# Low-part matmuls at the end of each block, 15 KB more of small tiles, and a ninth early expert chunk in a two-layer diffusion backbone

## The chip, the cores and the metric

The kernel runs on one core of a Trainium2 chip. The metric is the device time of one execution in microseconds. Matmuls run on TensorE (PE in the profile, its weight loads PEld), elementwise work on VectorE (DVE), ScalarE (ACT) and GpSimd (POOL); SyncE (SP) issues every transfer between device memory and the on-chip SBUF. Each engine works through its own queue in order and waits on semaphores for the others.

## The reference

Two layers over 256 latent tokens and 256 context tokens of width 1024. Cut to what matters here:

```python
def _layer(x, xc, sc, sc_ctx, p, lambda_init, ctx_out):
    mod = split(sc @ p['w_mod'] + p['b_mod'], 6)               # modc likewise for the context
    h  = modulate(rmsnorm(x,  p['norm1_g']), mod[0],  mod[1])
    hc = modulate(rmsnorm(xc, p['norm1_g']), modc[0], modc[1])
    y, yc = token_mixer(h, hc, p, lambda_init, ctx_out)
    x = x + mod[2] * y
    x = x + mod[5] * ec_moe(modulate(rmsnorm(x, p['norm2_g']), mod[3], mod[4]), p)
    ...                                                        # the context alike, in layer 0 only
def token_mixer(h, hc, p, lambda_init, ctx_out):
    dq, dk, dv, hy, sq, sk, sv, gt = split_in(h @ p['w_in'])   # w_in: 1024 x 10752
    ...          # differential attention, Hyena long convolution, windowed attention
    return merge([y_diff, y_hy, y_swa], gt, p)
def merge(ys, gate_pre, p):
    gs = split(sigmoid(gate_pre), 3)
    merged = sum(gs[b] * (ys[b] @ p['w_branch'][b]) for b in range(3))
    return merged @ p['w_out']
def ec_moe(h, p):                                              # 16 experts, each takes its 32 best tokens
    aff = softmax(h @ p['router_w'])
    g, idx = top_k(swapaxes(aff, 1, 2), 32)
    xg = h[idx]
    a, b = xg @ p['moe_w1'], xg @ p['moe_w3']
    return scatter_add(idx, (silu(a) * b) @ p['moe_w2'] * g)
```

All values are fp32. An expert has three matrices of 1024 x 1024, so a layer reads 16 x 3 x 4 MiB = 201 MB of expert weights.

## The kernel before

Each layer has a mixer stage and an expert stage.

**Mixer.** `run_blocks` (L998) works through 116 blocks a layer: 84 of w_in (128 output columns each), 24 of w_branch and 8 of w_out. A block's weights come as one raw tile of 512 KB (`load_block`, L971). `split_block` (L976) makes two tiles in TensorE's fast fp32 form out of it: `wh`, the rounded high part, by ScalarE, and `wl`, the remainder. GpSimd makes the second half of `wl` at once; VectorE's half (`rest`, L984) is held back in a list, `later`, and put into VectorE's queue towards the end of the block before. The activations are split likewise into `hi` and `lo` (`hhi`, `hlo` for w_in, `yb` for a branch, `mg` for w_out). The product of a block is the sum over eight k-tiles of three matmuls: `wh` with `hi`, `wh` with `lo`, `wl` with `hi` (`mm3`, L460). Every matmul loads its own stationary tile. 512 columns stand for latents and context, 256 for the latents alone, which most blocks of layer 1 need.

**Background.** The three token mixers, the modulation vectors and others are generators that a planner (`Background`, L287) puts between the matmuls of the blocks. When the program is built, a model keeps a clock for each engine; `pump` (L367) hands over the next background step when the model says that its operands are ready and a credit allows it, `until` (L383) does so while the model says that TensorE would wait for the tiles named, and `drain` forces a group to its end where a branch needs it. So the order of every engine's queue is fixed at build time. `LATER` (L39) says from which k-tile on a block releases the next block's `rest` and may request a further raw tile; a raw tile is requested ahead only while more than `SPARE` tiles of 4 KB are free (L1040).

**Experts.** The weights come in 96 chunks a layer of 2 MB (`fill`, L1664), in the order in which `prod` (L1829) consumes them, into seven tiles of 16 KB. Four of the first chunks are requested during the last mixer blocks of layer 0 (`PREF`, L46). Chunks named in `extra` (L1654) go into tiles of 4 KB and 2 KB that are free only at the start of the stage: chunk 4 into four of 4 KB (5 in layer 1), chunk 7 into three of 4 KB and two of 2 KB. The later ones wait until `prod` has used up a chunk.

**Memory.** `BUFS` (L58) holds the number of tiles of each size: a16 is 16 KB per partition, a4 4 KB, a2 2 KB, a1 1 KB. The program object reserves 16 KB per partition for descriptors of transfers that GpSimd issues.

Of the kernel before, what the change touches and what calls it, by code (L numbers as in the profile page):

```python
# [21 lines left out]
KT = 8  # L22
T = 256
L = 2
# [11 lines left out]
COST = {"setup": 500.0, "filter": 60000.0, "mod": 15000.0, "modA": 5000.0, "modN": 5000.0, "diff": 9000.0, "hy": 10000.0, "swa": 4000.0, "post": 1000.0}  # L36
CREDIT = (3000.0, 4000.0)
SLACK = 200.0
LATER = (6, 4)  # L39
SPARE = (1, 1)  # L40
EARLY = 1
FILTER_E = 4
# [12 lines left out]
ORDER = ("dddd" + "hhd" * 2 + "hhhh" + "dd", "dh" * 4 + "dddd")  # L55
PI_IN = 3.1415925
SWAP = list(range(16, 32)) + list(range(16))
BUFS = {"a16": 7, "a8": 3, "a4": 10, "a2": 8, "a1": 3, "t": 6, "s": 24, "t2": 1}  # L58


def constants():
# [347 lines left out]
class Kernel:  # L409
# [24 lines left out]
    def sb(self, tag, shape, dt=F32, name="w"):  # L434
        self.cnt += 1
        t = self.pool.tile(shape, dt, name=f"{name}_{self.cnt}", tag=tag, bufs=BUFS[tag])
        self.model.tile(t, tag, BUFS[tag])
        return t
# [559 lines left out]
    def run_blocks(self, bl, ahead=2, first=3):  # L998
        nl = ns = first
        later = []  # L1000
        for j, b in enumerate(bl):
            self.bg.due, end = [], self.bg.now
            for c in bl[j:]:
                if c.drains:
                    self.bg.due.append((c.drains, end))
                end += 24 * (4.0 + 0.41 * c.n)
            while ns < min(max(j + ahead, first + (j > 0)), len(bl)):
                self.split_block(bl[ns], later if j else None)
                ns += 1
            while nl < len(bl) and (nl <= ns or (nl - ns < 3 and self.model.dead("a4", BUFS["a4"]) > SPARE[self.bg.layer])):  # L1010
                self.load_block(bl[nl])
                nl += 1
            if self.bg.layer and len(bl) - 1 - j == MODR:
                self.bg.add("mod", lambda task: self.mod_vec([(1, v) for v in range(3, 6)]))
            if j < first:
                while later:
                    later.pop(0)()
                if j == 0:
                    for c in bl[:first]:
                        if c.pre:  # L1020
                            c.pre()
                    hi, lo = b.hl()
                    ps = [self.bank([128, c.n], "d" if i < 2 else "b") for i, c in enumerate(bl[:first])]
                    for k in range(KT):
                        self.bg.until([hi[:, k], lo[:, k]])
                        for c, p in zip(bl, ps):
                            self.mm3(p, (c.wh[:, k], c.wl[:, k]), (hi[:, k, 0:c.n], lo[:, k, 0:c.n]), k == 0, k == KT - 1)
                b.wh = b.wl = None
                b.evac(ps[j])
                continue  # L1030
            if b.pre:
                b.pre()
            hi, lo = b.hl()[:2]
            p = self.bank([128, b.n], "d")
            for k in range(KT):
                self.bg.until([b.wh[:, k], b.wl[:, k], hi[:, k], lo[:, k]])
                self.mm3(p, (b.wh[:, k], b.wl[:, k]), (hi[:, k, 0:b.n], lo[:, k, 0:b.n]), k == 0, k == KT - 1)
                if k >= LATER[self.bg.layer] and later:
                    later.pop(0)()
                if k > LATER[self.bg.layer] and nl < len(bl) and nl - ns < 3 and self.model.dead("a4", BUFS["a4"]) > SPARE[self.bg.layer]:  # L1040
                    self.load_block(bl[nl])
                    nl += 1
                if k < KT - 1:
                    self.bg.pump()
            b.wh = b.wl = None
            if len(bl) - 1 - j in PREF[self.bg.layer]:
                self.fill(PREF[self.bg.layer][len(bl) - 1 - j])
            b.evac(p)
            self.bg.pump()
# [21 lines left out]
    def clear(self, n):  # L1071
        while self.model.dead("a2", BUFS["a2"]) < n:
            self.bg.force()

    def room(self, **need):
        def gate():
            return all(self.model.dead(tag, BUFS[tag]) >= n for tag, n in need.items())
        return gate
# [547 lines left out]
    def moe(self, l):  # L1626
        nc, A = self.nc, self.A
        nq = 4 if l < L - 1 else 2
        ns = nq // 2
# [21 lines left out]
        self.mw = []  # L1651
        self.held, self.live = 0, deque()
        full = 6 if l < L - 1 else 7
        extra = {4: (4, 0, 1), 7: (3, 2, 2)} if l < L - 1 else {5: (4, 0, 1), 7: (3, 2, 2)}  # L1654

        def row(c, k):
            return c[:, k] if len(c.shape) == 3 else c[:, k // c.shape[2], k % c.shape[2]]
# [400 lines left out]
```

## Time and profile before

| | |
|---|---|
| median of 3 runs | 2607.61 us (2601.46 to 2608.32) |
| profiled execution | 2600.63 us, its span 2598.8 us |
| TensorE busy | 2244.1 us (86%), granted clock 0.943 on average |
| VectorE, ScalarE, GpSimd busy | 1338.3 (51%), 884.2 (34%), 793.6 us (31%) |
| transfers | 590.31 MB, 227 GB/s on average |

The page shows the whole execution; shares of busy time are averages over the stages, so the stages have to be read one by one. A row of the timeline gives an instruction's start and length and, in brackets, how long its engine was idle before it and who ended that. Matmuls are pipelined: the distance from one start to the next is their price, the length shown is more. The granted clock is the share of 2.4 GHz that TensorE was given; it has two levels, 2.4 and 1.2 GHz.

### The profile page before, as it was taken

The page shows a single profiled execution, that of the slowest core. Times are in us where ns is not written, and L with a number is a line of the kernel's source. Part 1 is how long each engine was busy: PE and PEld are TensorE (multiplying, and loading weights), DVE is VectorE, ACT ScalarE, POOL GpSimd, SP SyncE. Part 2 cuts the span into 40 slices and gives each one's busy share as a digit, 9 for nine tenths or more (in the row PEclk, how much of TensorE's full clock was granted, in tenths as well). Part 3 has the DMA queues.
Part 4 walks back from the last instruction along what each step waited for, and adds up shares of the span by engine and source line. Part 5 has one row for each costly group of instructions (what it writes and reads, how often), then busy time and mean ns, then how long its engine had stood idle before and what let it go on. Part 6 is the DMA issues. An engine that isn't in the chain of part 4 may idle for free.

```text
span 2598.8 us, 38727 instructions
## 1 busy us (share of the span) xinstructions
PE 2244.1 (86%) x14970; PEld 1539.4 (59%) x14970; DVE 1338.3 (51%) x2907; ACT 884.2 (34%) x1933; POOL 793.6 (31%) x775
## 2 busy tenths in 40 slices
PE   6999998999989998999998898988989887656565
PEld 4777776777768775333433377877877773223223
DVE  4777788788772324223333268778887541101011
ACT  4444444565552332101111154545544431000001
POOL 2644335642234540000111155664454430000000
PEclk8999999999999999999999999999999988788787
DMA  8443333221213367899999942322466689999997
GB/s 296 117 126 115 98 114 106 65 57 50 58 57 90 98 251 304 366 427 414 396 408 391 398 145 83 112 82 74 121 180 187 174 297 410 425 424 422 423 424 304
DMA packets 325983, 590.31 MB, mean 227 GB/s; under 512 B 45948, under 2 KB 278056, under 8 KB 297896
## 3 DMA queue, kind: packets, MB, share of 16 engines
q1 hardware_dynamic: 325800, 587.84, 61.8%
q8 instruction: 118, 1.93, 0.3%
q14 instruction: 65, 0.53, 0.1%
HBM read 584.66 MB, written 3.15 MB: 226 GB/s over the span
## 4 chain that ended last, share of the span: by engine, by line
PE 51%; DMA 22%; DVE 18%; ACT 3%; issue 3%; POOL 1%; SPq 1%; DVEq 0%; ACTq 0%; POOLq 0%
PE p L458 48%; DMA mw<-in_moe_w_dram 20%; DVE arena L261 6%; DVE t L261 4%; PE p L469 3%; DVE wl L261 2%; DMA wm<-in_w_mod_dram 2%; DVE qp L261 1%; SPq L261 1%; DVE yb L261 1%; ACT wh L261 1%; ACT arena L261 1%; DVE ma L261 1%; DVE yc L261 1%; ACT qp L261 1%
## 5 line engine op out<-in xcount | busy, mean ns | idle before, releaser
L458 PE MATMUL p<-mw,xg 128*32 128x256 f32 (+1 forms) x3072 | 412.4, 509 | 116.4 <-DMA mw<-in_moe_w_dram 114.0
L458 PE MATMUL p<-hhi,wl 128*128 128x512 f32 (+1 forms) x1344 | 480.4, 357 | 24.9 <-DVE wl L261 24.4
L458 PE MATMUL p<-hhi,wh 128*128 128x512 f32 (+1 forms) x1344 | 495.3, 369 | 7.2 <-ACT wh L261 4.1
L458 PE MATMUL p<-hlo,wh 128*128 128x512 f32 (+1 forms) x1344 | 476.4, 354 | 2.1 <-POOL hlo L261 1.3
L261 POOL TENSOR_TENSOR wl<-wraw,wh 128x512 fp32r<-128x512 f32 x232 | 343.0, 1479 | 392.2 <-ACT wh L261 320.7
L458 PEld LDWEIGHTS p<-mw,xg 128*32 128x32 f32 (+1 forms) x3072 | 133.1, 129 | 320.5 <-issue 201.8
L458 PEld LDWEIGHTS p<-hhi,wl 128*128 128x128 f32 x1344 | 258.6, 192 | 73.0 <-DVE wl L261 38.3
L458 PEld LDWEIGHTS p<-hhi,wh 128*128 128x128 f32 x1344 | 259.5, 193 | 43.9 <-issue 8.9
L458 PEld LDWEIGHTS p<-hlo,wh 128*128 128x128 f32 x1344 | 259.7, 193 | 30.0 <-POOL hlo L261 2.2
L261 ACT ACTIVATE wh<-wraw 128x1024 fp32r<-128x1024 f32 x232 | 242.4, 1053 | 50.8 <-DMA wraw<-in_w_in_dram 14.6
L458 PE MATMUL p<-mw,aT 128*32 128x256 f32 (+3 forms) x1760 | 197.1, 461 | 60.8 <-DMA mw<-in_moe_w_dram 57.9
L261 DVE TENSOR_TENSOR wl<-wraw,wh 128x512 fp32r<-128x512 f32 x231 | 198.6, 860 | 74.8 <-ACT wh L261 68.4
L261 ACT ACTIVATE arena<-p 128x512 f32<-128x512 f32 (+1 forms) x212 | 107.1, 509 | 374.2 <-PE p L458 290.3
L458 PE MATMUL p<-yb,wh 128*128 128x512 f32 (+1 forms) x768 | 196.7, 346 | 0.1
L458 PEld LDWEIGHTS p<-mw,aT 128*32 128x32 f32 (+1 forms) x1760 | 75.8, 128 | 171.3 <-issue 99.3
L261 DVE COPY yS<-p 32x512 f32<-32x512 f32 (+1 forms) x60 | 33.4, 556 | 268.9 <-ACT yS L261 268.9
L261 POOL TENSOR_TENSOR sq<-sq,sq 128x512 f32<-128x512 f32 (+1 forms) x6 | 6.3, 1055 | 506.4 <-ACT sq L261 502.9
L458 PE MATMUL p<-yb,wl 128*128 128x512 f32 (+1 forms) x384 | 133.0, 346 | 23.6 <-DVE wl L261 22.7
L458 PEld LDWEIGHTS p<-yb,wh 128*128 128x128 f32 x768 | 133.1, 194 | 15.7 <-issue 1.0
L261 ACT ACTIVATE arena<-p,t 128x512 f32<-128x512 f32 (+1 forms) x192 | 116.5, 613 | 66.4 <-DVE t L261 60.3
L261 ACT ACTIVATE s<-p 128x512 f32<-128x512 f32 (+1 forms) x32 | 15.7, 491 | 344.1 <-PE p L458 344.0
L261 ACT ACTIVATE yS<-p 32x256 f32<-32x256 f32 (+2 forms) x84 | 35.3, 420 | 261.5 <-PE p L458 233.9
(243 smaller groups left out, 3523.7 us busy)
## 6 DMA issues: line engine op xcount, KB each, us to landing
mw<-in_moe_w_dram SPq DMA_DIRECT2D x173, 2048.0 KB, 20.4
wraw<-in_w_in_dram SPq DMA_DIRECT2D x152, 512.0 KB, 3.9
wm<-in_w_mod_dram SPq DMA_DIRECT2D x72, 512.0 KB, 4.4
mw<-in_moe_w_dram SPq DMA_DIRECT2D x40, 512.0 KB, 22.5
mw<-in_moe_w_dram SPq DMA_DIRECT2D x17, 1024.0 KB, 29.2
wraw<-in_w_branch_dram SPq DMA_DIRECT2D x32, 512.0 KB, 3.7
wm<-in_w_mod_dram SPq DMA_DIRECT2D x5, 2048.0 KB, 7.9
wraw<-in_w_in_dram SPq DMA_DIRECT2D x32, 256.0 KB, 3.4
```

The costliest lines, as they stand in the source:

```text
L261: return f(*args, **kw)
L458: self.nc.tensor.matmul(out, lhsT=lhsT, rhs=rhs, start=start, stop=stop, skip_group_check=tiles > 1)
L469: self.nc.tensor.transpose(out, in_, self.ident[:n, :n])
```

## The change

Five places of the code change.

```diff
-LATER = (6, 4)
+LATER = (10, 6)
...
-BUFS = {"a16": 7, "a8": 3, "a4": 10, "a2": 8, "a1": 3, "t": 6, "s": 24, "t2": 1}
+BUFS = {"a16": 7, "a8": 3, "a4": 13, "a2": 9, "a1": 4, "t": 6, "s": 24, "t2": 1}
...
-            for k in range(KT):
-                self.bg.until([b.wh[:, k], b.wl[:, k], hi[:, k], lo[:, k]])
-                self.mm3(p, (b.wh[:, k], b.wl[:, k]), (hi[:, k, 0:b.n], lo[:, k, 0:b.n]), k == 0, k == KT - 1)
-                if k >= LATER[self.bg.layer] and later:
+            for i in range(2 * KT):
+                k = i % KT
+                if i < KT:
+                    self.bg.until([b.wh[:, k], hi[:, k], lo[:, k]])
+                    self.mm(p, b.wh[:, k], hi[:, k, 0:b.n], i == 0, False)
+                    self.mm(p, b.wh[:, k], lo[:, k, 0:b.n], False, False)
+                else:
+                    self.bg.until([b.wl[:, k]])
+                    self.mm(p, b.wl[:, k], hi[:, k, 0:b.n], False, k == KT - 1)
+                if i >= LATER[self.bg.layer] and later:
                     later.pop(0)()
-                if k > LATER[self.bg.layer] and nl < len(bl) and nl - ns < 3 and self.model.dead("a4", BUFS["a4"]) > SPARE[self.bg.layer]:
+                if i > LATER[self.bg.layer] and nl < len(bl) and nl - ns < 3 and self.model.dead("a4", BUFS["a4"]) > SPARE[self.bg.layer]:
                     self.load_block(bl[nl])
                     nl += 1
-                if k < KT - 1:
+                if i < KT or k % 2 and k < KT - 1:
                     self.bg.pump()
...
-        extra = {4: (4, 0, 1), 7: (3, 2, 2)} if l < L - 1 else {5: (4, 0, 1), 7: (3, 2, 2)}
+        extra = {4: (4, 0, 1), 7: (3, 2, 2), 8: (3, 2, 2)} if l < L - 1 else {5: (4, 0, 1), 7: (3, 2, 2), 8: (3, 2, 2)}
...
-    nc = bacc.Bacc("TRN2", target_bir_lowering=False, num_devices=1)
+    nc = bacc.Bacc("TRN2", target_bir_lowering=False, num_devices=1, dynamic_dma_scratch_size=1024)
```

A block now has 16 steps instead of 8: eight of two matmuls with `wh`, then eight of one with `wl`. The release of the next `rest` moves from step 6 of 8 (after 21 of 24 matmuls) to step 10 of 16 (after 19) in layer 0, and from after 15 to after 14 in layer 1. `pump` is called after the first eight steps and after three of the last eight. The first three blocks of a layer, which run together, keep the old order.

TensorE's queue at the first block of a branch product in layer 0 (`p_4815`, in the changed program `p_4881`), before:

```order
L458 MATMUL p_4815<-yb_4760,wh_4756 128x512
L458 MATMUL p_4815<-yb_4761,wh_4756 128x512
L458 MATMUL p_4815<-yb_4760,wl_4757 128x512
...
L458 MATMUL p_4827<-kp_4382,qp_4720 128x256
L458 MATMUL p_4827<-kl_4383,qp_4720 128x256
```

and now (`yb_4829` is the high part of the branch's activations, `yb_4830` the low part; the `arena` and `cst` rows are background; left out are repeats of the two `wh` rows):

```order
L458 MATMUL p_4881<-yb_4829,wh_4823 128x512
L458 MATMUL p_4881<-yb_4830,wh_4823 128x512
L469 MATMUL p_4884<-cst_68,arena_575 128x128 x2
...
L458 MATMUL p_4907<-arena_575,arena_573 128x128 x2
...
L458 MATMUL p_4917<-arena_575,arena_574 128x128 x4
...
L458 MATMUL p_4881<-yb_4829,wl_4824 128x512 x6
L469 MATMUL p_4936<-cst_68,arena_574 128x128 x4
L458 MATMUL p_4881<-yb_4829,wl_4824 128x512 x2
```

The third matmul used `wl`; now the eight with `wl` stand at the end, and the matmul that reads `arena_573` comes after five pairs of `wh` matmuls. VectorE's queue at the same place, before:

```order
L261 TENSOR_TENSOR yb_4761<-arena_575,yb_4760 128x512
L261 TENSOR_TENSOR yb_4761<-arena_576,yb_4760 128x512 x3
L261 TENSOR_TENSOR wl_4757<-wraw_4542,wh_4756 128x512
L261 TENSOR_TENSOR qp_4720<-arena_574,qp_4720 64x128 x2
L261 TENSOR_REDUCE t_4838<-p_4827 128x1
```

and now:

```order
L261 TENSOR_TENSOR yb_4830<-arena_573,yb_4829 128x512
L261 TENSOR_TENSOR yb_4830<-arena_574,yb_4829 128x512 x2
L261 TENSOR_TENSOR yb_4830<-arena_573,yb_4829 128x512
L261 TENSOR_TENSOR wl_4824<-wraw_4557,wh_4823 128x512
L261 COPY arena_573<-p_4884 128x256
L261 RECIPROCAL t_4793<-t_4793 128x2
```

`wl` stands behind the four `yb` instructions in both; what follows it is other background work. SyncE's queue at the start of layer 0's expert stage, where `mw` are tiles of expert weights, before:

```order
L261 DMA mw_8935<-in_moe_w_dram 128x1024
L261 DMA mw_8939<-in_moe_w_dram 128x512
L261 DMA mw_8940<-in_moe_w_dram 128x512
L261 DMA mw_9095<-in_moe_w_dram 128x4096
L261 DMA mw_9105<-in_moe_w_dram 128x4096
```

and now:

```order
L261 DMA mw_8939<-in_moe_w_dram 128x512
L261 DMA mw_8940<-in_moe_w_dram 128x512
L261 DMA mw_8943<-in_moe_w_dram 128x1024
L261 DMA mw_8944<-in_moe_w_dram 128x1024
L261 DMA mw_8945<-in_moe_w_dram 128x1024
L261 DMA mw_8949<-in_moe_w_dram 128x512
L261 DMA mw_8950<-in_moe_w_dram 128x512
L261 DMA mw_9105<-in_moe_w_dram 128x4096
```

Chunk 8, one transfer into a tile that a used-up chunk has to free (`mw_9095`), became five into small tiles (`mw_8943` to `mw_8950`); chunk 9 now takes the first freed tile.

## Rows read from the trace of the kernel before

**Rows 1.** Table of stretches: start and end, length, busy us of each engine, clock, DMA.

```profile
41.00:780.00 739.00, 693.82 (x3893) 534.51 (x3892) 565.73 (x1263) 368.01 (x843) 322.83 (x346) 0.98 0.32 92
...
1510.00:2030.00 520.00, 462.94 (x3176) 406.98 (x3175) 409.65 (x804) 273.04 (x547) 276.16 (x245) 0.96 0.39 114
2130.00:2600.00 470.00, 299.10 (x3619) 142.29 (x3619) 67.01 (x187) 41.30 (x114) 2.85 (x4) 0.82 0.96 399
```

**Rows 2.** Costly groups of the page: busy, mean ns, idle before and its releaser.

```profile
L458 PE MATMUL p<-hhi,wl 128*128 128x512 f32 (+1 forms) x1344 | 480.4, 357 | 24.9 <-DVE wl L261 24.4
L458 PE MATMUL p<-yb,wl 128*128 128x512 f32 (+1 forms) x384 | 133.0, 346 | 23.6 <-DVE wl L261 22.7
```

**Rows 3.** Waits of TensorE, 41 to 985 us: total us, times, longest us.

```profile
PE p L458 <- DVE wl L261: 25.7, 23, 4.2
PE p L469 <- DVE arena L261: 3.5, 7, 1.2
```

**Rows 4.** Waits of TensorE, 1500 to 2130 us.

```profile
PE p L458 <- DVE wl L261: 21.4, 14, 3.9
PE p L469 <- DVE arena L261: 16.0, 16, 2.5
PE p L469 <- DVE yd L261: 13.7, 5, 4.2
PE p L458 <- ACT wh L261: 4.1, 2, 3.3
```

**Rows 5.** Timeline of TensorE, 748 to 756 us: start, length, instruction, idle before.

```profile
748.30 0.39 PE L458 MATMUL p<-hlo,wh 128*128 128x512 f32 x1
748.53 0.39 PE L458 MATMUL p<-hhi,wl 128*128 128x512 f32 x1
...
753.54 0.80 PE L458 MATMUL p<-yb,wl 128*128 128x512 f32 x1 [4.16 <-DVE wl L261]
754.13 1.05 PE L458 MATMUL p<-yb,wh 128*128 128x512 f32 x2
754.99 0.63 PE L458 MATMUL p<-yb,wl 128*128 128x512 f32 x1
```

**Rows 6.** Timeline of TensorE in layer 1, 2039 us.

```profile
2039.21 0.28 PE L458 MATMUL p<-hlo,wh 128*128 128x256 f32 x1
2039.33 0.28 PE L458 MATMUL p<-hhi,wl 128*128 128x256 f32 x1
```

**Rows 7.** Timeline of VectorE, then of TensorE, 519 to 526 us.

```profile
519.02 5.21 DVE L261 TENSOR_TENSOR yb<-arena,yb 128x512 fp32r<-128x512 f32 x4
524.15 1.75 DVE L261 TENSOR_TENSOR wl<-wraw,wh 128x512 fp32r<-128x512 f32 x1
...
525.96 0.54 PE L458 MATMUL p<-yb,wl 128*128 128x512 f32 x1 [3.44 <-DVE wl L261]
```

**Rows 8.** Table of stretches behind waits for wl, first and last.

```profile
274.00:277.00 3.00, 3.00 (x14) 1.24 (x13) 3.00 (x4) 1.45 (x4) 2.92 (x4) 0.50 0.57 176
...
2079.00:2082.00 3.00, 3.00 (x15) 3.00 (x16) 1.78 (x2) 0.00 (x0) 1.96 (x2) 0.56 0.99 243
```

**Rows 9.** DMA queues of the page: packets, MB, share of 16 engines' span.

```profile
q1 hardware_dynamic: 325800, 587.84, 61.8%
```

**Rows 10.** Table of stretches in the expert stages; last three numbers clock, DMA, GB/s.

```profile
1005.00:1010.00 5.00, 4.54 (x31) 4.00 (x31) 2.39 (x11) 0.00 (x0) 0.00 (x0) 0.50 0.97 404
1015.00:1020.00 5.00, 5.00 (x42) 2.40 (x40) 2.81 (x12) 2.56 (x8) 0.00 (x0) 1.00 0.01 3
2140.00:2145.00 5.00, 5.00 (x77) 2.98 (x78) 2.64 (x11) 2.77 (x8) 0.00 (x0) 0.92 0.02 5
2160.00:2165.00 5.00, 5.00 (x80) 3.20 (x73) 1.87 (x7) 1.39 (x4) 0.00 (x0) 1.00 1.00 424
```

**Rows 11.** Waits of TensorE for expert weights, 985 to 1500, then 2130 to 2600 us.

```profile
PE p L458 <- DMA mw<-in_moe_w_dram: 20.6, 21, 2.0
...
PE p L458 <- DMA mw<-in_moe_w_dram: 151.4, 80, 5.7
```

## Prediction

> **What bounds the kernel now.** I read the table of stretches first, with stretches cut where the program changes its work [rows 1]. The reader is to see two kinds. In the two mixer stretches (41 to 780 and 1510 to 2030 us) TensorE is busy 94% and 89% of the time, VectorE 77% and 79%, and the DMA engines a third: a mixer ends when TensorE's stream of matmuls ends, and VectorE is near enough behind it to hold it up. In an expert stretch (the second, 2130 to 2600 us) the DMA share is 0.96 while TensorE falls to 64%: there the weights' arrival sets the end.
>
> Then the page's list of costly groups, for what ended TensorE's idle time [rows 2]. The groups that read `wl`, the low part of a weight block, were preceded by 24.9 us of idle time in the w_in blocks and 23.6 us in the branch blocks, nearly all of it ended by VectorE writing `wl`. The lists of waits say where: 25.7 us in 23 waits before 985 us [rows 3], 21.4 us in 14 waits from 1500 to 2130 us [rows 4]; together 47.1 us, the longest 4.2 us. Last the timelines of single waits and the stretches behind them, for the clock and for what VectorE was doing.
>
> The sum below is made against the profiled execution's own 2600.63 us (a span of 2598.8 us and 1.83 us around it). That execution is 7.0 us under the median of the three runs, 2607.61 us, so I add 7 at the end.
>
> **The change part by part.**
>
> *Low-part matmuls last.* Counts stay: 24 matmuls a block, each with its own weight load, before and after. What moves is when `wl` is first needed. Before, it was the third matmul of a block; now it is the seventeenth, so 14 matmuls stand between. With 512 columns one starts every 0.23 us (748.30 and 748.53 us in [rows 5]), with 256 every 0.12 us [rows 6]: 3.2 us or 1.7 us of grace. The waits average 25.7/23 = 1.1 us and 21.4/14 = 1.5 us, so nearly every one is shorter than the grace it gets. VectorE's instruction for `wl` keeps its place behind the background work in its queue, so its end does not move.
>
> That bounds the gain at 47 us. The other bound is that VectorE is simply late: TensorE works in order, and once past `wl` it meets a background matmul that needs VectorE too. The branch block shown in the order listing tells how much. VectorE finished four `yb` instructions at 524.2 us and `wl` at 525.9 us; TensorE stood 3.44 us before the block's third matmul, until 525.96 us [rows 7]. In the new order the sixth pair is preceded by a matmul on `arena_573`, which VectorE copies right behind `wl`: TensorE gets 10 matmuls (2.3 us) into the block instead of 2, and about half of the wait is left there. So I take half of the branch blocks' 22.7 us, 11 us, and 70% of the w_in blocks' 24.4 us, 17 us, since those waits are shorter and a block of w_in has no `yb` instructions in front of its `wl`. Together **28 us**; bounds 12 (a quarter) and 47.
>
> *The clock behind those waits.* After seven of the waits the granted clock was at 1.2 GHz, half, for some microseconds; first and last of the seven are [rows 8], and the row at 753.54 us in [rows 5] shows it: after 4.16 us of waiting, two matmuls take 0.86 us, not 0.46. Seven stretches of 3 us (one of 6) with a mean clock near 0.52 lose about 24 x 0.48 = 11.5 us. Where the wait halves, the fall may still come: I take 60%, **7 us**; bounds 2 and 11.5. Where the clock falls elsewhere, I leave it.
>
> *More pump points and thresholds.* A block now hands over to the background tasks after 11 of its steps, before after 7, so the same background matmuls come in smaller portions and partly earlier. No instruction is added; I count zero here and put the risk into the rivals.
>
> *Small tiles.* 13, 9 and 4 tiles in place of 10, 8 and 3 of the sizes 4, 2 and 1 KB: 15 KB per partition, paid for by the scratch. Raw weight blocks can be requested earlier. TensorE waited 4.1 us for `wh` in two places in the second layer [rows 4], one of them 3.27 us with the clock halved behind it; an earlier request removes most: **3 us**; bounds 0 and 6.
>
> *Scratch of 1 KB.* All of the program's own transfers stand on one hardware queue [rows 9] and are issued by SyncE; GpSimd issues none. Nothing uses what is taken away: 0 us.
>
> *Ninth early chunk.* A chunk is 128 x 4096 fp32 = 2.10 MB; at the 424 GB/s that the queue reaches [rows 10] that is 4.95 us. Both expert stretches have a hole to put it in: the queue moved 3 GB/s from 1015 to 1020 us and 5 GB/s from 2140 to 2145 us, because every buffer was full [rows 10]. Filling it moves all later chunks forward by up to 4.95 us. In the second layer TensorE waits 151.4 us for these weights [rows 11], so the end follows in full. In the first it waits only 20.6 us, so a little is lost: 4 us. Together **9 us**; bounds 4.9 and 9.9. The chunk comes in five transfers (three of 512 KB, two of 256 KB) where the later ones are one of 2 MB. From 1005 to 1010 us, while two whole and two split chunks were being worked off, the queue still ran at 404 GB/s [rows 10], so I charge nothing for the splitting. The Trainium skill (SBUF — State Buffer, "The DMA setup-cost knee") speaks against the piece: a transfer pays about 2 us whatever its size, so the largest single transfer is to be preferred. By that rule four more transfers would cost an estimated 8 us each time if nothing hid them, 16 us in all, and the sum would come out at 2576 us; the 404 GB/s disagrees as long as transfers are queued behind each other.
>
> **Sum.** 28 + 7 + 3 + 9 = 47 us; 2600.6 - 47 = 2553.6, plus 7: **2560 us**. With all lower bounds, 12 + 2 + 0 + 5 = 19, it is 2589; with all upper ones, 47 + 11.5 + 6 + 10 = 74.5, it is 2533.
>
> **The rivals.**
>
> *The wait only moves.* If VectorE sets the pace of the mixers, all of the 47 us and the clock loss come back in front of background matmuls. For it: VectorE is 79% busy in the second mixer, and TensorE's other long waits there, 16.0 us for `arena` and 13.7 us for `yd` [rows 4], are already VectorE being late. Against it: in the first layer the waits for `arena` are 3.5 us [rows 3], so VectorE mostly catches up. Only the chunk and the raw loads stay: 2607.6 - 12 = 2596 us.
>
> *Slower.* The place is the mixers' background matmuls: with more pump points they may be put into TensorE's stream before their operand is ready, and everything behind stands. Its price is read from what they cost now: 3.5 us [rows 3] and 16.0 + 13.7 us [rows 4], 33.2 us. It decides from the point where the growth of these exceeds what `wl`, clock, raw loads and chunk give. If they grow by three quarters, 25 us, while the `wl` waits come back as well: 2596 + 25 = 2621 us. Against it speaks that the same number of matmuls is spread over more places, not bunched.
>
> *The ninth chunk buys nothing*, because the thirteen 4 KB tiles it needs are still held by the last w_out blocks, or TensorE's gather stands in the way. Then 47 - 9 = 38 us remain: 2569 us.
>
> *More than the sum.* The extra small tiles also let background tasks start earlier, and half of those 33.2 us go too, and some 8 us of half clock behind them: 2560 - 25 = 2535 us.
>
> **How the numbers follow.** Forecast 0.56, the wait only moves 0.16, slower 0.06, chunk without effect 0.14, more than the sum 0.08. The forecast's own range is 2533 to 2589 us. The range of 8 in 10 has to take in most of the first rival (2596) and leaves out the far ends: 2530 to 2602 us. A measurement of this kernel can tell about 0.3% from no change, here 7.8 us, so faster means under 2599.8 us. Faster is the forecast, the idle chunk, the larger gain and 0.09 of the moved wait: 0.87. Same is 0.07 of the moved wait and 0.01 of the slower case: 0.08. Slower is the remaining 0.05.
>
> **What would show it.** Right: TensorE's waits for `wl` fall from 47 us to under 15 us; its waits for `arena` and `yd` grow by less than 20 us; the stretches of half clock behind branch blocks' third matmul are gone; the first expert weight is needed some 30 to 40 us earlier in each profile's own time; in the few microseconds after each router the queue stays above 300 GB/s. The forecast is wrong in its main step if the `wl` waits vanish and the mixers are as long as before: then VectorE paced them. It is wrong in the chunk if the two expert stretches, measured from the first expert matmul to the end, are not shorter by 4 to 5 us each.

## The result and the profile after

The changed kernel takes 2577.82 us (median of 4 runs, 2572.00 to 2579.04) against 2605.77 us for the kernel before in the same comparison: a ratio of 0.9893, 95% interval 0.9878 to 0.9908. That is 28 us faster; forecast were 47 from the profiled time. The pair of profiles shows less, 2600.63 - 2579.04 = 21.6 us, because the profiled run of before was faster than all its timed runs and that of after was the slowest of its four.

First the stretches: before, then after, cut at the same points of the program (first block, first branch product, first w_out block of layer 0; the same for layer 1, there up to the last branch block). These four rows of before are finer than [rows 1].

```profile
41.00:522.00 481.00, 453.87 (x2471) 351.40 (x2471) 370.59 (x751) 226.14 (x483) 244.11 (x255) 0.97 0.37 111
522.00:940.00 418.00, 397.68 (x2128) 312.69 (x2127) 239.08 (x575) 186.45 (x422) 150.64 (x139) 0.99 0.26 75
1514.00:1814.00 300.00, 269.55 (x1681) 238.09 (x1682) 227.52 (x464) 164.34 (x319) 174.97 (x151) 0.98 0.32 90
1814.00:2093.00 279.00, 243.84 (x1898) 219.88 (x1898) 212.94 (x384) 130.95 (x263) 134.33 (x121) 0.94 0.58 165
```

```profile
42.00:526.00 484.00, 453.34 (x2488) 352.12 (x2488) 377.82 (x768) 233.27 (x502) 240.73 (x257) 0.98 0.37 111
526.00:933.00 407.00, 392.05 (x2111) 308.63 (x2110) 231.55 (x558) 179.50 (x403) 151.71 (x136) 1.00 0.28 81
1508.00:1787.00 279.00, 260.25 (x1643) 229.55 (x1642) 232.38 (x438) 157.76 (x302) 167.89 (x147) 0.99 0.33 95
1787.00:2071.00 284.00, 253.10 (x1937) 229.86 (x1936) 217.36 (x409) 135.09 (x280) 144.91 (x125) 0.92 0.57 163
```

Layer 0 gained 8 us (899 to 891), layer 1 16 us (579 to 563). Layer 1's w_in part gained 21 and its branch part lost 5. The counts of matmuls (x, first column) move between the parts: background work is shifted, so only a whole mixer can be compared.

The groups of after that answer to [rows 2], and two that grew (columns: busy, mean ns, idle before and its releaser):

```profile
L458 PE MATMUL p<-hhi,wl 128*128 128x512 f32 (+1 forms) x1344 | 312.9, 361 | 4.5 <-DVE wl L261 4.4
L458 PE MATMUL p<-yb,wl 128*128 128x512 f32 (+1 forms) x384 | 79.1, 343 | 0.1
L469 PE MATMUL p<-cst,arena 128*128 128x128 f32 x608 | 101.0, 290 | 28.8 <-DVE arena L261 27.8
L458 PE MATMUL p<-kp,qp 128*128 128x512 f32 (+1 forms) x192 | 75.3, 399 | 12.2 <-DVE qp L261 11.3 <-ACT arena L261 0.4
```

The waits for `wl` are gone: 4.4 us are left of 47.1. Where TensorE waits now, layer 0 (42 to 979 us) and then layer 1 (1494 to 2109 us), against [rows 3] and [rows 4]:

```profile
PE p L469 <- DVE arena L261: 10.2, 12, 3.0
PE p L458 <- DVE qp L261: 6.6, 9, 2.0
PE p L458 <- DVE arena L261: 6.4, 4, 3.0
PE p L458 <- POOL yb L261: 5.9, 9, 1.6
PE p L469 <- DVE yd L261: 3.2, 4, 1.7
...
PE p L469 <- DVE arena L261: 17.6, 16, 2.8
PE p L458 <- DVE arena L261: 8.2, 5, 3.3
PE p L469 <- DVE yd L261: 4.9, 2, 4.0
PE p L458 <- DVE qp L261: 4.7, 6, 2.3
PE p L458 <- DVE wl L261: 4.4, 4, 2.9
```

In layer 0 much of the 25.7 us came back before `arena`, `qp` and `yb`: TensorE's gaps over 0.3 us add up to 47 us before and 46 after. In layer 1 they fell from 64 to 47 us, `yd` alone from 13.7 to 4.9. At the block of [rows 7] two operands are late now: first `yb` itself, which I had not counted, and then, five pairs of matmuls into the block, the `arena` tile that I had argued with (timeline of TensorE, then VectorE's `wl`, after):

```profile
525.74 0.62 PE L458 MATMUL p<-yb,wh 128*128 128x512 f32 x2
...
526.34 0.48 PE L458 MATMUL p<-yb,wh 128*128 128x512 f32 x1
528.40 1.18 PE L458 MATMUL p<-yb,wh 128*128 128x512 f32 x4 [1.58 <-POOL yb L261]
530.10 0.97 PE L458 MATMUL p<-yb,wh 128*128 128x512 f32 x3 [0.52 <-POOL yb L261]
532.66 0.71 PE L458 MATMUL p<-arena,arena 128*128 128x128 f32 x4 [1.60 <-DVE arena L261]
...
530.52 1.76 DVE L261 TENSOR_TENSOR wl<-wraw,wh 128x512 fp32r<-128x512 f32 x1
```

The waits inside this block are 1.58 + 0.52 + 1.60 = 3.7 us, against 3.44 us before: here nothing of the wait is gained. The queue in the expert stages, answering to [rows 10] (last number GB/s): the hole behind each router is still there, and layer 0 has a second one.

```profile
1009.00:1014.00 5.00, 5.00 (x41) 2.40 (x42) 2.75 (x11) 2.52 (x8) 0.00 (x0) 1.00 0.02 5
1046.00:1051.00 5.00, 5.00 (x54) 3.50 (x52) 1.55 (x5) 1.28 (x4) 0.00 (x0) 0.97 0.00 0
1051.00:1056.00 5.00, 5.00 (x46) 2.45 (x43) 2.46 (x9) 2.23 (x8) 0.00 (x0) 1.00 0.00 0
2109.00:2114.00 5.00, 0.69 (x4) 0.23 (x4) 4.03 (x14) 0.42 (x1) 0.67 (x1) 0.50 1.07 425
2119.00:2124.00 5.00, 5.00 (x63) 2.91 (x64) 1.76 (x7) 1.86 (x7) 0.00 (x0) 0.75 0.03 7
```

At the second hole the kernel before still moved 59 and then 360 GB/s:

```profile
1052.00:1057.00 5.00, 5.00 (x57) 3.50 (x55) 1.55 (x5) 1.28 (x4) 0.00 (x0) 1.00 0.25 59
1057.00:1062.00 5.00, 5.00 (x46) 2.46 (x43) 2.45 (x9) 2.21 (x8) 0.00 (x0) 1.00 0.86 360
```

From the first to the last expert matmul, layer 0 takes 480.6 us before and 481.5 after, layer 1 445.1 and 444.9.

### The profile page after: what moved, and what is told of

Read it like the earlier page. It is cut to its first block, busy times and chain, and to the rows that moved or that the text cites. A ratio compares the mean times of both kernels' runs of the same rounds, so it can differ in the third digit from the quotient of the medians.

```text
span 2577.3 us, 38619 instructions
## 1 busy us (share of the span) xinstructions
PE 2240.2 (87%) x14970; PEld 1542.7 (60%) x14970; DVE 1347.2 (52%) x2907; ACT 882.1 (34%) x1933; POOL 794.8 (31%) x775
## 4 chain that ended last, share of the span: by engine, by line
PE 47%; DMA 20%; DVE 20%; issue 4%; ACT 4%; POOL 3%; SPq 1%; DVEq 0%; POOLq 0%; ACTq 0%
PE p L458 44%; DMA mw<-in_moe_w_dram 19%; DVE arena L261 6%; DVE t L261 5%; PE p L469 3%; DVE wl L261 2%; DVE qp L261 2%; ACT arena L261 1%; DMA wm<-in_w_mod_dram 1%; POOL wl L261 1%; SPq L261 1%; POOL arena L261 1%; DVE ma L261 1%; DVE yc L261 1%; ACT wh L261 1%
## 5 line engine op out<-in xcount | busy, mean ns | idle before, releaser
L458 PE MATMUL p<-mw,xg 128*32 128x256 f32 (+1 forms) x3072 | 411.0, 508 | 115.3 <-DMA mw<-in_moe_w_dram 114.4
L458 PE MATMUL p<-hhi,wh 128*128 128x512 f32 (+1 forms) x1344 | 471.4, 363 | 10.1 <-DVE arena L261 7.7
L458 PE MATMUL p<-hlo,wh 128*128 128x512 f32 (+1 forms) x1344 | 458.9, 354 | 1.6 <-POOL hlo L261 0.8
L458 PEld LDWEIGHTS p<-mw,xg 128*32 128x32 f32 (+1 forms) x3072 | 133.7, 129 | 317.1 <-issue 200.0
L458 PE MATMUL p<-hhi,wl 128*128 128x512 f32 (+1 forms) x1344 | 312.9, 361 | 4.5 <-DVE wl L261 4.4
L458 PEld LDWEIGHTS p<-hhi,wh 128*128 128x128 f32 x1344 | 259.4, 193 | 48.5 <-issue 13.3
L458 PEld LDWEIGHTS p<-hlo,wh 128*128 128x128 f32 x1344 | 259.6, 193 | 31.4 <-POOL hlo L261 1.7
L458 PE MATMUL p<-mw,aT 128*32 128x256 f32 (+3 forms) x1760 | 200.4, 475 | 62.5 <-DMA mw<-in_moe_w_dram 58.2
L261 DVE TENSOR_TENSOR wl<-wraw,wh 128x512 fp32r<-128x512 f32 x231 | 217.0, 940 | 57.4 <-ACT wh L261 47.0
L458 PEld LDWEIGHTS p<-hhi,wl 128*128 128x128 f32 x1344 | 222.0, 194 | 37.0 <-DVE wl L261 5.2
L458 PEld LDWEIGHTS p<-mw,aT 128*32 128x32 f32 (+1 forms) x1760 | 79.5, 134 | 172.3 <-issue 109.0
L458 PE MATMUL p<-yb,wh 128*128 128x512 f32 (+1 forms) x768 | 153.6, 343 | 7.5 <-POOL yb L261 6.8
L458 PEld LDWEIGHTS p<-yb,wh 128*128 128x128 f32 x768 | 118.5, 190 | 26.8 <-POOL yb L261 11.6
L469 PE MATMUL p<-cst,arena 128*128 128x128 f32 x608 | 101.0, 290 | 28.8 <-DVE arena L261 27.8
```

Of the source, the lines that this page charges most:

```text
L261: return f(*args, **kw)
L458: self.nc.tensor.matmul(out, lhsT=lhsT, rhs=rhs, start=start, stop=stop, skip_group_check=tiles > 1)
L469: self.nc.tensor.transpose(out, in_, self.ident[:n, :n])
```

## The experiments

All runs in one table; the lengths are from each kernel's trace, in us. "Mixer" runs from the layer's first block to its first w_out block (layer 0) or last branch block (layer 1), "experts" from the first to the last expert matmul. "Run" is an unbroken run of over 100 background matmuls in layer 0 and its length. Ratios are to the kernel before, in the comparison that each run was part of.

| kernel | wl last in layer | run in layer 0 | mixer 0 | mixer 1 | experts 0, 1 | median, ratio and interval |
|---|---|---|---|---|---|---|
| before | none | none | 899.1 | 579.1 | 480.6, 445.1 | 2605.77 |
| after | 0, 1 | none | 891.1 | 563.2 | 481.5, 444.9 | 2577.82, 0.9893 [0.9878, 0.9908] |
| e_order | 0, 1 | 45.6 | 920.3 | 565.1 | 483.5, 448.5 | 2609.22, 1.0015 [1.0003, 1.0026] |
| e_tiles | none | none | 909.8 | 578.9 | 481.3, 446.1 | 2612.85, 1.0025 [1.0013, 1.0038] |
| e_nochunk | 0, 1 | none | 892.1 | 561.5 | 476.5, 445.7 | 2576.97, 0.9889 [0.9871, 0.9908] |
| e_new1 | 1 | none | 909.1 | 558.4 | 480.8, 444.8 | 2592.08, 0.9947 [0.9930, 0.9964] |
| e_a4only | 0, 1 | 39.0 | 912.7 | 566.0 | 478.1, 446.0 | 2600.52, 0.9979 [0.9966, 0.9992] |
| e_slack | 0, 1 | none | 897.1 | 564.9 | 479.7, 444.5 | 2579.50, 0.9904 [0.9881, 0.9927] |
| e_order_slack | 0, 1 | as e_order | 920.0 | 565.4 | 480.1, 446.1 | 2608.16, 1.0019 [1.0009, 1.0028] |
| e_pump7 | 0, 1 | none | 895.2 | 566.8 | 479.5, 442.8 | 2581.84, 0.9919 [0.9904, 0.9933] |
| e_order_rate | 0, 1 | none | 883.9 | 564.5 | 484.3, 445.9 | 2573.69, 0.9890 [0.9869, 0.9910] |
| e_small | 0, 1 | none | 891.8 | 564.4 | 481.3, 446.1 | 2595.96, 0.9962 [0.9949, 0.9974] |
| e_backlog | 0, 1 | none | 890.6 | 566.9 | 480.6, 440.1 | 2579.63, 0.9899 [0.9885, 0.9914] |
| e_rate | none | 42.4 | 940.1 | 578.8 | 483.5, 448.6 | 2643.87, 1.0147 [1.0129, 1.0166] |

Several kernels share a plan: by the names and shapes in the traces, TensorE, VectorE, ScalarE and GpSimd each run the same instructions in the same order. In layer 0's mixer these are after, e_nochunk, e_small and e_backlog (890.6 to 892.1 us); e_order and e_order_slack; e_tiles and e_new1. In layer 1's they are after, e_nochunk, e_new1 and e_slack (558.4 to 564.9 us); e_order, e_order_slack and e_order_rate; before and e_rate. So one plan's mixer repeats within 1.5 us in layer 0 and 6.5 us in layer 1, and smaller differences show nothing.

**e_order**: the new loop and `LATER`, the rest as before.

```diff
-LATER = (6, 4)
+LATER = (10, 6)
 BUFS = {"a16": 7, "a8": 3, "a4": 10, "a2": 8, "a1": 3, "t": 6, "s": 24, "t2": 1}
```

> Only the order of the low-part matmuls, its pump points and LATER; tiles, scratch and the chunk as before. Theory 1, the grace: the long way from a block's first matmul to its first wl is what pays, so most of the gain stays, about 24 of the 28 us, a time near 2582 us, and TensorE's waits for wl are under 10 us. Rival, the tiles: the extra small tiles, by which raw weights come earlier, pay in layer 1, so this kernel gains only layer 0's part, about 8 us, a time near 2598 us, and TensorE waits for wl or wh in layer 1.

2609.22 us: no gain at all, which neither theory had. TensorE's waits for `wl` fell to 6.8 us, and layer 1 did as the grace theory said (14 us), but layer 0 became 21 us longer. One place in layer 0 stands out, in the table of stretches, then the groups of TensorE inside it:

```profile
522.00:567.60 45.60, 29.27 (x156) 22.07 (x155) 33.23 (x104) 24.63 (x71) 8.74 (x14) 0.74 0.08 24
```

```profile
L458 PE MATMUL p<-kp,qp 128*128 128x256 f32 (+1 forms) x12 | 6.8, 571 | 1.5 <-DVE qp L261 0.8 <-ACT qp L261 0.6
L469 PE MATMUL p<-cst,arena 128*128 128x128 f32 x30 | 5.8, 330 | 7.1 <-DVE arena L261 7.1
...
L458 PE MATMUL p<-arena,svt 128*64 128x128 f32 x40 | 3.8, 317 | 0.5 <-DVE arena L261 0.3 <-ACT arena L261 0.2
L458 PE MATMUL p<-yf,ft 128*128 128x256 f32 x12 | 3.3, 443 | 0.4 <-POOL yf L261 0.4
L469 PE MATMUL p<-cst,yd 128*128 128x128 f32 x8 | 1.7, 357 | 3.6 <-DVE yd L261 3.6
```

For 45.6 us TensorE has 154 background matmuls between two of weight blocks (the row's 156); at the distances at which matmuls of their shapes start elsewhere in this trace (lower quartile) they would take about 14 us. TensorE stands idle for 16 us there, 14 of them before an operand that VectorE makes, and the granted clock is 0.74 on average. By the code and the place this is `drain`: a branch begins, Hyena's group isn't done, and the planner forces it (`yf`) to its end, with whatever else is ready (`qp`, `svt`, `yd`). That this run is what costs the 21 us is tested by e_order_rate and e_small below.

**e_tiles**: tiles and scratch only.

```diff
-BUFS = {"a16": 7, "a8": 3, "a4": 10, "a2": 8, "a1": 3, "t": 6, "s": 24, "t2": 1}
+BUFS = {"a16": 7, "a8": 3, "a4": 13, "a2": 9, "a1": 4, "t": 6, "s": 24, "t2": 1}
```

> Only the 13, 9 and 4 small tiles and the scratch of 1 KB; old order of matmuls, no ninth chunk. The grace: a gain of about 3 us, 2603 us, TensorE's waits for wl still 35 us or more. The tiles: a gain of 15 us or more, 2590 us or less, and the waits for wl in layer 1 halved.

2612.85 us: slower. Layer 1 is unchanged to 0.2 us, so the tiles give nothing by themselves; layer 0's plan is 10.7 us longer without a forced run (TensorE's longest list of waits but `wl` is `arena`, 12.0 us against 3.5).

**e_nochunk**: after, without the ninth chunk.

```diff
-extra = {4: (4, 0, 1), 7: (3, 2, 2), 8: (3, 2, 2)} if l < L - 1 else {5: (4, 0, 1), 7: (3, 2, 2), 8: (3, 2, 2)}
+extra = {4: (4, 0, 1), 7: (3, 2, 2)} if l < L - 1 else {5: (4, 0, 1), 7: (3, 2, 2)}
```

> The changed kernel without the ninth early chunk. By my forecast the chunk gave 9 us, so 2587 us, and the last expert matmul comes 4 to 5 us later against the first one in each layer. By the reading of the two traces it gave nothing in layer 0, where a second hole of the queue 35 to 50 us after the router grew by what the first one saved, and 4 us of earlier arrival in layer 1 that the end did not use: 2578 to 2582 us.

2576.97 us: the chunk gave no time that can be measured. It did its work in the queue all the same: without it the queue runs dry 5 to 6 us sooner, and the hole behind the router is longer by that. The row of after that follows the one at 2109 us shown above, then the two of e_nochunk at the same distances from the first expert matmul (2119.2 and 2114.2 us):

```profile
2114.00:2119.00 5.00, 4.11 (x33) 3.74 (x33) 2.30 (x9) 0.38 (x2) 0.00 (x0) 0.50 0.74 313
```

```profile
2104.00:2109.00 5.00, 0.64 (x3) 0.21 (x4) 4.09 (x14) 0.42 (x1) 0.67 (x1) 0.50 0.59 249
2109.00:2114.00 5.00, 4.11 (x33) 3.77 (x33) 2.30 (x9) 0.50 (x2) 0.00 (x0) 0.50 0.00 0
```

In layer 1 its bytes did come early: SyncE issues the last transfer of weights 428.3 us after the first expert matmul with the chunk, 433.0 without. The last 20 us show what became of it, after (from 2551 us) and e_nochunk (from 2547 us), both some 432 us behind the first expert matmul; the clock stands third from the end of a row:

```profile
2551.00:2561.00 10.00, 5.79 (x203) 4.65 (x200) 1.76 (x4) 3.81 (x15) 0.73 (x1) 0.84 0.55 174
2561.00:2571.00 10.00, 9.68 (x112) 8.20 (x110) 4.52 (x18) 6.15 (x18) 1.46 (x2) 0.79 0.01 2
```

```profile
2547.00:2557.00 10.00, 6.25 (x197) 4.24 (x197) 1.76 (x4) 3.34 (x12) 0.72 (x1) 1.00 0.88 279
2557.00:2567.00 10.00, 8.94 (x145) 7.46 (x145) 4.72 (x19) 6.50 (x20) 1.45 (x2) 1.00 0.03 9
```

The weights are there sooner (174 against 279 GB/s still to come), but in this execution TensorE ended at a clock of 0.8, and the 4 us were gone. The other kernels with the chunk bear that out: counted from 425 us behind the first expert matmul, TensorE is at half clock for 13.0 to 13.4 us in after, e_new1 and e_slack (experts 444.5 to 444.9 us), for 7.8 us in e_pump7 (442.8) and for 1.6 us in e_backlog (440.1). What decides the clock there wasn't tried. Over all profiles layer 1's experts take 443.4 us with the chunk (mean of 5) and 446.5 without (mean of 9): some 3 us. In layer 0 it is 480.4 and 481.0.

**e_new1**: after, with the old loop and old `LATER` in layer 0.

```diff
-LATER = (10, 6)
+LATER = (6, 6)
...
+            if self.bg.layer == 1:
...
+            else:
+                for k in range(KT):
...
```

> The changed kernel with the old order of matmuls (and the old LATER) in layer 0, the new order in layer 1 alone. If the two layers' gains are independent and go as in the profiles (8 us in layer 0's mixer, 16 in layer 1's), the time is near 2586 us. If layer 0's new order gains nothing, since what wl gives up there comes back as waits for arena, qp and yb, it is 2578 us. If layer 0 carries the gain, 2595 us or more.

2592.08 us, between the first and the third expectation: both layers gain. Layer 0's mixer is 909.1 us, the plan and the length of e_tiles, so the expected 8 us were too few: against after the new order is worth 18 us in layer 0 with these tiles. In layer 1 it is worth 16 to 20 us (e_tiles 578.9; the one plan of after and e_new1 took 563.2 and 558.4).

**e_a4only**: e_order with thirteen 4 KB tiles (and the scratch of 1 KB that makes room, as in e_small below).

```diff
-BUFS = {"a16": 7, "a8": 3, "a4": 10, "a2": 8, "a1": 3, "t": 6, "s": 24, "t2": 1}
+BUFS = {"a16": 7, "a8": 3, "a4": 13, "a2": 8, "a1": 3, "t": 6, "s": 24, "t2": 1}
```

> The new order with thirteen tiles of 4 KB, but 8 and 3 of 2 and 1 KB as before, and no ninth chunk. If the new order costs 21 us in layer 0 because the ten 4 KB tiles run out (they hold raw, high and low parts of the weights), these three tiles alone bring layer 0's mixer back to about 891 us and the time to about 2578 us. If layer 0's length is a matter of which plan the planner happens to make, layer 0's mixer may be anywhere from 880 to 920 us and the time from 2568 to 2608 us; layer 1's mixer stays at 558 to 566 us by both.

2600.52 us: the 4 KB tiles aren't what layer 0 lacks. The forced run is still there, 39 us long.

**e_slack**: after with another tolerance, and **e_order_slack**: the same edit on e_order.

```diff
-SLACK = 200.0
+SLACK = 150.0
```

> The changed kernel with SLACK, a tolerance of the planner, at 150 in place of 200: nothing that has a price changes, only the plan. If tiles and order have their worth by themselves, the time stays at 2578 us within 4 us and layer 0's mixer at 891 us within 3 us. If layer 0 is a matter of the plan, its mixer differs from 891 us by 5 us or more, in either direction.

> The new order alone (old tiles, no ninth chunk) with SLACK at 150. If the ten 4 KB tiles are what costs 21 us in layer 0, its mixer stays near 920 us and the time near 2609 us. If the plan is, its mixer differs from 920 us by 8 us or more, likely downwards, towards 2595 us.

2579.50 and 2608.16 us. In the first the plan of layer 0 changes and its mixer becomes 6 us longer, so by the sign that I had set the plan counts, by some microseconds. In the second the edit changes nothing: the plan is that of e_order in both mixers. That run only repeats e_order; it doesn't test the tiles against the plan, and my suspicion that layer 0 is a matter of the plan stays open until e_order_rate.

**e_pump7**: after with seven pump points a block.

```diff
-                if i < KT or k % 2 and k < KT - 1:
+                if i % 2 and i < 2 * KT - 1:
```

> The changed kernel with seven pump points a block, as before the change, in place of eleven. My forecast put the extra points at zero: 2578 us. If the finer portions are part of the gain, 2585 us or more; if they do harm (they let background matmuls in before VectorE has their operands), 2570 us or less, with fewer waits for arena.

2581.84 us, between the first two expectations; its interval overlaps that of after. The two mixers are 4.1 and 3.6 us longer, no more than other plans differ by (6 us in e_slack). So the extra points give a few microseconds or nothing; no harm shows.

**e_order_rate**: e_order with a faster hand-over in layer 0.

```diff
-RATE = (0.75, 0.6)
+RATE = (1.0, 0.6)
```

> The new order alone (old tiles, old scratch, no ninth chunk) with the planner's RATE of layer 0 at 1.0 in place of 0.75, so that background steps are handed over sooner and Hyena's group is done before its drain. Theory, the drain: the order alone lost its gain in layer 0 to one run of 154 background matmuls that took 45.6 us at 522 us with no weight block in between; without that run layer 0's mixer falls from 920 us to 885 to 895 us and the time from 2609 to about 2580 us, with the old tiles. Rival, the tiles: they are needed for something else, layer 0's mixer stays over 905 us and the time over 2595 us.

2573.69 us, with the old tiles, the old scratch and no ninth chunk. The forced run is gone and layer 0's mixer fell by 36.4 us, to 883.9, a little below what was expected; layer 1 kept e_order's plan and length (565.1 and 564.5 us).

**e_small**: e_order with 9 and 4 tiles of 2 and 1 KB, ten of 4 KB.

```diff
-BUFS = {"a16": 7, "a8": 3, "a4": 10, "a2": 8, "a1": 3, "t": 6, "s": 24, "t2": 1}
+BUFS = {"a16": 7, "a8": 3, "a4": 10, "a2": 9, "a1": 4, "t": 6, "s": 24, "t2": 1}
```

> The new order with ten tiles of 4 KB as before, but 9 and 4 of 2 and 1 KB, and no ninth chunk. By the theory of the drain the plan of this kernel has no run of forced Hyena matmuls in layer 0, so its mixer takes 885 to 897 us there, as with all the tiles. If the three 4 KB tiles matter by themselves (raw weights requested earlier), it stays over 905 us. Layer 1's mixer is 560 to 572 us.

Layer 0's mixer is 891.8 us and has no forced run: the two small tiles are enough. They even give layer 0 the very plan of after, so there the three 4 KB tiles change nothing in the order; that the scratch alone does it is ruled out by e_a4only, which has the same scratch. The time is 2595.96 us all the same, because this kernel stalls elsewhere, before the modulation vectors in front of layer 1's w_out (table of stretches, then TensorE's wait in it):

```profile
2072.00:2091.70 19.70, 1.89 (x12) 1.04 (x13) 9.64 (x12) 2.47 (x3) 3.05 (x3) 0.62 0.77 237
```

```profile
PE p L458 <- DVE ma L261: 17.4, 1, 17.4
```

**e_backlog**: after with a larger backlog allowed in layer 1.

```diff
-BACKLOG = (1500.0, 750.0)
+BACKLOG = (1500.0, 1500.0)
```

> The changed kernel with the planner's BACKLOG of layer 1 at 1500 ns in place of 750: background steps are handed over although ScalarE or VectorE is modelled up to 1.5 us behind. The plan then has no forced drain of sliding-window tasks at the end of layer 1's mixer, where the changed kernel ran 228 background matmuls in 39.2 us (28.5 us more than their own pace). Theory, the drain costs what it waits: layer 1's mixer falls from 563 us to 540 to 550 us, the time to 2555 to 2566 us. Rival, VectorE paces layer 1: the waits come back in front of the matmuls put in earlier, and the time stays at 2574 us or more.

2579.63 us: the theory of the drain fails in layer 1. After has a run of 228 background matmuls there, before one of 190 in 33.9 us (the row of after; counted as in e_order, their own pace is 14 us, so the run's excess is 25 us, not the 28.5 of the expectation):

```profile
1985.00:2024.20 39.20, 30.29 (x229) 23.27 (x229) 30.73 (x85) 22.53 (x62) 4.90 (x9) 0.83 0.10 27
```

In e_backlog it is gone, and the two parts of layer 1's mixer take:

```profile
1508.00:1806.00 298.00, 272.54 (x1697) 240.17 (x1697) 247.18 (x475) 170.08 (x332) 175.68 (x155) 0.98 0.33 92
1806.00:2075.00 269.00, 244.76 (x1885) 221.72 (x1885) 199.90 (x371) 123.77 (x249) 137.52 (x121) 0.92 0.59 174
```

The branch part is 15 us shorter than in after and the w_in part 18 us longer. VectorE's work in the w_in part grew from 232.4 to 247.2 us, and it is 83% busy there in both. But TensorE has 54 more matmuls there too, and its busy time grew from 260.3 to 272.5 us; only 6.7 us of the 19 between the two rows are more idle time. The rival's time came true (2574 us or more); that VectorE paces this part isn't shown, since most of what it gained in length is TensorE's own moved work.

**e_rate**: before with the faster hand-over of e_order_rate.

> The kernel before with RATE of layer 0 at 1.0 and nothing else: the old order of matmuls, no run of forced Hyena matmuls in either plan. If the order is what gains, in layer 0 as in layer 1, layer 0's mixer stays at 895 to 905 us and the time at 2606 us within 6 us. If the faster hand-over is the gain of the kernel with the new order and this rate (884 us in layer 0), and the order itself gives nothing there, layer 0's mixer is 880 to 890 us and the time near 2590 us.

2643.87 us, outside both expectations, because their premise was wrong: this plan does have a forced run in layer 0.

```profile
539.00:581.40 42.40, 26.83 (x163) 20.43 (x163) 31.91 (x107) 21.74 (x64) 6.87 (x11) 0.80 0.04 13
```

With the old order the rate brings the run, with the new one it removes it. So the rate by itself isn't the gain of e_order_rate, and the run costs the old order about as much, 940.1 - 899.1 = 41 us, as it cost the new one (36.4).

**Together.** Each plan counted once, with the mean of its runs: in layer 0, plans without the forced run take 904 us with the old order (two plans, 899 and 909) and 892 with the new (four plans, 884 to 897), so the order gives 12 us. With the run it is 940.1 (one plan) and 916 (two plans). Layer 1 takes 579 us with the old order (two plans) and 565 with the new (six plans, 562 to 567): 14 us. Between plans of the same kind the order is worth some 26 us, and in e_order one forced run takes all of it back. Two plans of the old order are few, but no old one is as short as a new one of its kind. Why a plan gets the run was not followed; two small tiles or a faster hand-over remove it from the new order, and the faster hand-over brings it into the old. No kernel here is measurably faster than after; e_order_rate equals it without the tiles, the scratch or the chunk.

## Why the prediction was right, and where it was not

**Direction, range and the main cause** were right. The order is what pays, and what I booked for it, 28 + 7 us, stands against some 26 us measured between plans of the same kind, 24 in this pair of profiles. That the direction came out, however, was in part luck: with the order alone the kernel is 2.5 us slower (e_order), and the tiles that saved it I had booked for another reason.

**Low-part matmuls.** The waits for `wl` fell below 15 us (4.4), and those for `arena` and `yd` at L469 didn't grow in sum: 33.2 us in [rows 3, 4], 10.2 + 17.6 + 3.2 + 4.9 = 35.9 now, 3.2 of it a row of layer 0 that I had not counted before (3.3 there). What I missed is `qp` (5.9 to 11.3), `yb` from GpSimd (none to 6.9) and `arena` at L458 (5.7 to 14.6). "About half of the wait is left" was wrong at the one block that I had read: the 1.60 us before `arena` are the half that I had worked out, but 2.1 us before `yb` came on top, which I had put at nothing. That the end of `wl` does not move was wrong there too: VectorE finished it at 532.28 us, 6.5 us after the block's first matmul, 4.0 us before the change. The split by kind of block can't be held against the trace, since background work moved between the parts.

**The clock.** No half clock follows a branch block's third matmul any more, but it appears elsewhere: 35 to 22 us in layer 0's mixer, 44 to 48 in layer 1's. With half of the speed lost that is 0.5 x (13.5 - 3.4) = 5 us of my 7.

**Small tiles: the step that failed.** I booked them as an independent 3 us for earlier raw weights. The waits for `wh` in layer 1 that I had booked them on are gone in every kernel with thirteen 4 KB tiles and 0.4 to 5.8 us in those with ten, but that shortens nothing: alone the tiles give 0.2 us in layer 1's mixer and cost 10.7 us in layer 0's. What they do is to keep a forced run of Hyena out of the new order's plan, worth 28.5 us there (920.3 in e_order, 891.8 in e_small), and the 2 KB and 1 KB tiles are the ones that do it. I added up the terms of edits that meet in one planner; the sum of the two alone would have been 2.5 + 6.1 = 8.6 us slower, together (e_nochunk, in the same comparison) they are 29.8 us faster. That the plan could fall into a forced run stood in no rival.

**Ninth chunk: wrong, by the sign that I had named.** The expert stretches aren't 4 to 5 us shorter. The holes after the routers look as before (5 and 7 GB/s), though SyncE issued the chunk's five transfers in time (991.1 to 1001.3 us and 2102.0 to 2107.5 us) and e_nochunk shows that they keep the queue busy for 5 to 6 us longer. What I had missed is that the tiles widen the hole first: over all traces the queue stands still behind the routers (gaps of over 0.9 us) for 9 to 12 us with thirteen 4 KB tiles and no ninth chunk, 4 to 9 us with ten, and 4 to 7 us with thirteen and the chunk. The chunk fills about what the tiles had opened. In layer 0 the next thing to stop the queue is a tile that TensorE hasn't used up, and a second hole grew by what was gained (12 us against 5 in before and 4 in e_nochunk); in layer 1 about 3 of 4.95 us reach the end on average, and 0.2 us between the profiles of before and after. My rival "the ninth chunk buys nothing" came true in another way than I wrote: the tiles were free and the transfers early.

**Splitting** cost nothing that shows: while the chunk's five transfers were worked off, the queue moved 425 GB/s (row at 2109 us). The Trainium skill (SBUF — State Buffer, "The DMA setup-cost knee") charges about 2 us to every transfer; by it four more, with nothing to hide them, would have shown as an estimated 8 us. The trace disagrees for transfers that stand queued.

**Where the 18 us between 2560 and 2578 went**: in the profiled pair the chunk is short by 10 us (9 booked, 0.7 us longer), the mixers by 14 (38 booked, 24 found) and the stretches between the stages by 2, about 25 us in all. Some 8 us of that come back on the way to the medians: I had added 7 us for them, and the median of after lies 1.2 us under its profiled run. The first expert weight is needed 21.3 us earlier, not 30 to 40. The rival "the wait only moves" describes layer 0 in this pair (gaps 47 to 46 us, the gain is clock), not layer 1.

## What to carry to other kernels

Where a planner sets the order, don't add up the effects of edits, and check that an edit of its constants changes the order at all, since e_order_slack's changed nothing. Look in each plan for long runs of background work without a main matmul, since one such run of 40 us can hide all that an edit gains. Moving a late operand's use to the end of a block pays what the wait was, less what the next late operand takes; list that one too. Freeing buffers for one more early transfer pays only if the consumer, too, has nothing else to wait for at the end.

## What the runs showed of the hardware

TensorE's clock fell to half behind single waits of 1.9 us (1.86 us before the matmul at 1618.47 us in after, 1.88 us before the one at 529.79 us in e_tiles). It also fell at 321.5 us in before with no wait just before it: since 318.23 us TensorE had been running 32 background matmuls of 128x16 one behind the other. The same plan repeats itself to within 1.5 us in layer 0 (four kernels, 890.6 to 892.1 us) and 6.5 us in layer 1 (four kernels, 558.4 to 564.9). VectorE's `wl` instruction, the same in all kernels, takes 839 to 869 ns on average where both layers have the old order and 894 to 945 where both or layer 1 have the new one (231 of them; 18 us more of VectorE between before and after). The traces show where: with no GpSimd instruction running beside it, it takes 685 ns in before (78 of them) and in after (82); with GpSimd running throughout, 1006 ns in before (93) and 1230 in after (92). So the longer time lies in what GpSimd does at the same moment; no run was made on it. Why e_tiles' plan of layer 0 is 10.7 us longer than that of before stays open.
